# Where GpSimd's three side stores stand: one loop with a comparison, and tiles 16 and 23 in 5, 48 and 75 partitions

## The chip, the cores and the metric

The kernel runs on one core of a Trainium2 chip. The metric is the device time of one execution in microseconds; for the kernel before it is the median of three runs, 207.06 us (207.04 to 207.12). The core has five engines with programs of their own: TensorE (PE in the profile), VectorE (DVE), ScalarE (ACT), GpSimd (POOL) and SyncE (SP). They meet through semaphores. Transfers between the chip's main memory (HBM) and the on-chip memory (SBUF, 128 partitions) are issued by SyncE and by GpSimd and carried out by 16 DMA engines.

## The reference

```python
"x": (16, 512, 1024) float32, "weight": (1024, 768) float32, "add_value": (16, 512, 768) float32, scale = 0.1

return (scale * np.matmul(x, weight) + add_value).astype(np.float32)
```

Read as one matrix, x has 8192 rows. 33.6 MB of x, 25.2 MB of add_value and 3.1 MB of the weight are read, and 25.2 MB are written.

## The kernel before, in words

The 8192 rows are 64 tiles of 128 rows, one row a partition. Sixteen consecutive rows belong to one partition (`R = 16`), so a tile range such as "(8, 8)", tiles 8 to 15, is one contiguous piece of HBM for each partition. A name like x(40,8) below is the entry `("x", 40, 8)` of the list `STREAM` (L22): the load of tiles 40 to 47 of x. a(40,8) loads the same tiles of add_value, and o(40,8) would store them.

SBUF holds x in 16 tile slots (`xs`), and add_value in 32 slots (`ao`), which are also where the results are made and from where they are stored. Tile t uses slot t mod 16 of `xs` and slot t mod 32 of `ao`. The weight comes in through slots 24 to 31 of `ao`.

Five programs run side by side.

- SyncE (`sync_engine`, L97) issues the entries of `STREAM` in the order written there, each after the waits that it needs: a load of x into a used slot waits until ScalarE and GpSimd have cast what was in it (`by_act`, `by_pool`); a load of add_value waits for the load of add_value before it (`a_sem`), for the store that frees its slots (`o_sem`), and, where its slots hold the tile `PAIR.start`, for GpSimd's stores (`aside_sem`, L125); a store waits for the second last store before it (`o_sem`) and until its last tile is finished (`made`). SyncE does one entry after the other, so an entry that waits holds up all entries behind it.
- ScalarE and GpSimd (`mover`, L150) cast x to bf16, each one half of every tile. A turn of their loop is 16 tiles, in four groups of four tiles; each group is eight casts on each of the two engines. The group waits for its load (`x_sem`) and until its buffer `va` has been transposed (`turned`).
- VectorE (`vector_engine`, L166) transposes two tiles at a time (`turn`, `xt` from `va`) and finishes two tiles at a time (`finish`: scale times product plus add_value, in place in `ao`). In its order the transposes of tiles 40 and 41 stand between the finishing of tiles 36, 37 and that of tiles 38, 39.
- TensorE (`tensor_engine`, L218) multiplies tile by tile, four tiles a turn, and has four accumulators.

Around the change: GpSimd's program before is the loop of `mover` for the first two turns (tiles 0 to 31), a wait until tile 15 is finished (`made`, L246), three stores over GpSimd's own DMA queue (`store_pair`, L93), an alignment of the instruction address (`addr_align`, L249), and the loop again for the last two turns. The three stores carry tiles 8 and 15 (`PAIR = slice(8, 16, 7)`) in 6, 98 and 24 partitions (`BY_POOL`: partitions 122 to 127, 0 to 97 and 98 to 121). SyncE stores the tiles between them, 9 to 14, as o(9,6), and tiles 16 to 23 as o(16,8). The load that takes the slot of tile 8 again, and so waits for `aside_sem`, is a(40,8).

`addr_align(HALF_BLOCK, offset=PAST, max_nops=0)` places the instruction that follows it at 4 past a multiple of 64 instructions. ScalarE and VectorE have one ahead of their programs (L235).

Of the kernel before, what the change touches and what calls it, by code (L numbers as in the profile page):

```python
# [10 lines left out]
R = 16  # L11
X_SLOTS = 16
A_SLOTS = 32
# [6 lines left out]
HALF_BLOCK, PAST, SYNC_AT = 64, 4, 4  # L20
# [1 line left out]
STREAM = [  # L22
# [6 lines left out]
]  # L29
FIRST, ENDING = (0, 8), 48  # L30
PAIR, TURN_AT = slice(8, 16, 7), 2
BY_POOL = [(122, 6), (0, 98), (98, 24)]


@with_exitstack
def kernel(
# [8 lines left out]
    nc = tc.nc  # L45
# [8 lines left out]
    T = M // P  # L54
# [5 lines left out]
    out_v = out_f.rearrange("(g p t) n -> p g t n", p=P, t=R)  # L60
    w_v = weight.rearrange("(c p r) n -> p c (r n)", p=P, r=2)

    def rows(view, s, n):
        assert s // R == (s + n - 1) // R
        return view[:, s // R, s % R:s % R + n, :]
# [5 lines left out]
    ao = const.tile([P, A_SLOTS, N], fp32, name="ao")  # L71
# [10 lines left out]
    aside_sem = tc.alloc_semaphore("aside")  # L82
    by_act, by_pool, pool_go, turned, casts, done, made = (
        tc.alloc_semaphore(name)
        for name in ("by_act", "by_pool", "pool_go", "turned", "casts", "done", "made"))
    TURNED = MOVE * VA_BUFS
    MADE = TURNED + 2 + MM_BUFS - 2
# [3 lines left out]
        return t % A_SLOTS  # L91

    def store_pair(eng, p, n):  # L93
        assert PAIR.stop <= R and PAIR.stop <= A_SLOTS
        eng.dma_start(out_v[p:p + n, 0, PAIR, :], ao[p:p + n, PAIR, :]).then_inc(aside_sem, 16)  # L95

    def sync_engine(eng):  # L97
        groups, stores, known = 0, [], {}

        def need(sem, value):  # L100
            if known.get(sem, 0) < value:
                eng.wait_ge(sem, value)  # L102
                known[sem] = value

        for at, (op, s, n) in enumerate(STREAM):
# [14 lines left out]
            elif op == "a":  # L120
# [4 lines left out]
                if s <= PAIR.start + A_SLOTS <= last:  # L125
                    need(aside_sem, 16 * len(BY_POOL))
                if s >= A_SLOTS:
# [19 lines left out]
            if op == "x" and n == 2 * MOVE:  # L147
                eng.sem_inc(x_sem[k // MOVE + 1], 16)

    def mover(eng, copy, parity, count, go=None, first=0, turns=T // X_SLOTS):  # L150
        if go is None:
            eng.preload_act_table(mybir.ActivationFunctionType.Copy)  # L152
        with eng.Fori(16 * (first + 1), 16 * (first + turns) + 1, 16) as i:  # L153
            for q in range(X_SLOTS // MOVE):
                eng.wait_ge(x_sem[q], i)
                eng.wait_ge(turned, i + (4 * q - 12) if q < 3 else i)  # L156
                if go is not None:
                    eng.sem_inc(go, 1)  # L158
                k = MOVE * q
                src = xs[:, k:k + MOVE, :].rearrange("p i (c b k) -> p (i c) b k", b=4, k=64)  # L160
                for a in (parity, parity + 2):
                    for b in range(4):
                        copy(va[q % VA_BUFS][32 * b:32 * b + 32, :, a, :],  # L163
                             src[32 * a:32 * a + 32, :, b, :]).then_inc(count, 1)

    def vector_engine(eng):  # L166
        ao_g = ao.rearrange("p (g t) n -> p g t n", t=G)

        def cast_w(s, n):
            eng.wait_ge(w_sem[s // 4], 16)  # L170
            eng.tensor_copy(w_bf[:, s:s + n, :], ao[:, W_AT + s:W_AT + s + n, :]).then_inc(casts, n)  # L171

        def turn(move, half, moves=None):
            if half == 0:
                eng.wait_ge(by_act, moves)
                eng.wait_ge(by_pool, moves)  # L176
            q = 2 * half * KC
            eng.transpose(  # L178
                xt[:, 2 * half:2 * half + 2, :, :].rearrange("p i c m -> p (i c m)"),
                va[move % VA_BUFS][:, q:q + 2 * KC, :, :].bitcast(fp32).rearrange("p c a k -> p (c a k)"),  # L180
            ).then_inc(turned, 2)

        def finish(pair, at, products):
            eng.wait_ge(done, products)
            a = ao_g[:, at, 2 * pair:2 * pair + 2, :]
            q = 2 * (pair % 2)
            eng.scalar_tensor_tensor(  # L187
                a, mm[:, q:q + 2, 0:N], float(scale), a,
                op0=mybir.AluOpType.mult, op1=mybir.AluOpType.add).then_inc(made, 2)

        def group(i, at, last):
            eng.wait_ge(a_sem, i)
            for p in range(4):
                finish(p, at, i + (4 * p - 12) if p < 3 else i)
                if p < 2 or not last:
                    turn(1 if p < 2 else 0, p % 2, i + 8 if p == 2 else i)

        cast_w(0, 4)
        cast_w(4, 4)
        turn(0, 0, 8)  # L200
        turn(0, 1)
        with eng.Fori(16, 2 * T, 16) as i:
            group(i, bass.ds((i // 16 + A_SLOTS // G - 1) % (A_SLOTS // G), 1), False)
        s = slot(T - G) // G
        group(2 * T, slice(s, s + 1), True)
# [12 lines left out]
    def tensor_engine(eng):  # L218
        eng.sem_inc(x_sem[1], 16)
        eng.sem_inc(turned, TURNED)  # L220
        eng.sem_inc(made, MADE)
        eng.wait_ge(casts, KJ)
        with eng.Fori(TURNED + 2, TURNED + 2 + T, XT_TILES) as i:
            for q in range(XT_TILES):
                if q % 2 == 0:
                    eng.wait_ge(turned, i + q if q else i)
                    eng.wait_ge(made, i + q if q else i)
                for j in range(KJ):
                    x2 = xt[:, q, j // 2, :].bitcast(bf16).rearrange("p (m r) -> p r m", r=2)
                    m = product(eng, mm[:, q, :], x2[:, j % 2, :], w_bf[:, j, :], j)  # L230
                if q % 2:
                    m.then_inc(done, 4)


    for eng in (nc.scalar, nc.vector):  # L235
        eng.addr_align(HALF_BLOCK, offset=PAST, max_nops=0)
    s, n = FIRST
    place = dataclasses.replace(xs[:, s:s + n, :], dep_tracking_offset=P * X_SLOTS * K)
    first = nc.sync.dma_start(place, rows(x_v, s, n))
    first.then_inc(x_sem[0], 16)  # L240
    tc.no_tile_sem_insts.add(first.ins.name)
    with tc.tile_critical(no_gpsimd_drain=True):  # L242
        sync_engine(nc.sync)
        mover(nc.scalar, nc.scalar.copy, 0, by_act)
        mover(nc.gpsimd, nc.gpsimd.tensor_copy, 1, by_pool, pool_go, 0, TURN_AT)
        nc.gpsimd.wait_ge(made, MADE + PAIR.stop)  # L246
        for p, n in BY_POOL:
            store_pair(nc.gpsimd, p, n)
        nc.gpsimd.addr_align(HALF_BLOCK, offset=PAST, max_nops=0)  # L249
        mover(nc.gpsimd, nc.gpsimd.tensor_copy, 1, by_pool, pool_go, TURN_AT, T // X_SLOTS - TURN_AT)  # L250
        vector_engine(nc.vector)
        tensor_engine(nc.tensor)
    ctx.close()
# [39 lines left out]
```

## Time and profile before

| | |
|---|---|
| median of three runs | 207.06 us (207.04 to 207.12) |
| the profiled execution, in all | 206.85 us |
| its span, first to last instruction | 205.5 us |
| TensorE busy | 167.5 us, 82% |
| ScalarE, GpSimd busy | 134.7 us, 137.4 us |
| VectorE busy | 98.0 us |
| moved by DMA | 87.04 MB, 424 GB/s over the span |
| granted TensorE clock, mean | 0.986 |

The profile is of one execution. Times in its views count from the start of the span. "q1" is the queue of SyncE's transfers, "q0" that of GpSimd's, "q14" the queue by which engines fetch instructions. A row of the timeline has its start, its length, the engine ("SPq" is the issuing of SyncE), line, operation, what it writes and reads, how many, and in brackets how long the engine had stood idle and what ended that. A row of the DMA issues ends with the size of one transfer and the time from issue to landing. In the table by stretch each row has the stretch, its length, then busy time and count of instructions of PE, PEld, DVE, ACT and POOL, then clock, the DMA engines' mean busy share and what they moved in GB/s.

### The profile page before, as it was taken

What the parts mean: (1) busy time and instruction counts of PE and PEld (TensorE: products, weight loads), DVE (VectorE), ACT (ScalarE), POOL (GpSimd) and SP (SyncE); (2) the same over time, 40 slices, a digit from 0 to 9 for tenths busy, and PEclk for the clock granted to TensorE, in tenths of its full rate; (3) what the DMA queues carried; (4) which work ended last, traced back from release to release, by engine and by line L of the source; (5) the groups of instructions that cost most, each with busy time, mean ns of one, the idle gap of its engine ahead of it and who ended that gap; (6) DMA issues with size and microseconds to landing.
All of it is one profiled execution on the core that took longest, in us unless ns stands there. A gap on an engine that the chain in (4) does not pass through costs nothing.

```text
span 205.5 us, 2223 instructions
## 1 busy us (share of the span) xinstructions
PE 167.5 (82%) x1008; PEld 50.4 (25%) x512; DVE 98.0 (48%) x66; ACT 134.7 (66%) x129; POOL 137.4 (67%) x135
## 2 busy tenths in 40 slices
PE   0000099999999999999999999999999997999900
PEld 0000022233322333223332233332333322333200
DVE  0004525537555555465555555555552853455330
ACT  2049980699999906999999059999991099920000
POOL 0049994699999916999999549999992099930000
PEclk9999999999999999999999999999999999999995
DMA  8989999999999899999999999999999999998997
GB/s 287 427 372 438 440 485 408 392 437 459 446 459 459 357 459 408 408 426 413 455 404 450 431 416 464 434 411 421 440 431 415 437 448 421 493 459 364 423 440 304
DMA packets 4065, 87.04 MB, mean 424 GB/s; under 512 B 480, under 2 KB 480, under 8 KB 1120
## 3 DMA queue, kind: packets, MB, share of 16 engines
q1 hardware_dynamic: 3856, 86.25, 98.1%
q0 software_dynamic: 208, 0.79, 0.9%
q14 instruction: 1, 0.01, 0.0%
HBM read 61.87 MB, written 25.17 MB: 424 GB/s over the span
## 4 chain that ended last, share of the span: by engine, by line
DMA 38%; PE 36%; POOL 10%; ACT 5%; issue 4%; DVE 3%; SPq 1%; POOLq 0%; DVEq 0%; ACTq 0%
PE mm L210 36%; DMA out_dram<-ao 22%; DMA xs<-in_x_dram 15%; POOL va L163 9%; ACT va L163 5%; DVE xt L178 2%; DVE ao L187 1%; POOL out_dram L95 1%; SPq L130 0%; SPq L118 0%; DVEq L176 0%; SPq L102 0%; POOLq L156 0%; POOLq L158 0%; POOLq L153 0%
## 5 line engine op out<-in xcount | busy, mean ns | idle before, releaser
L210 PE MATMUL mm<-w_bf,xt 128*128 128x256 bf16 (+1 forms) x1008 | 167.5, 327 | 28.0 <-DVE xt L178 27.1
L163 POOL CAST va<-xs 32x1024 bf16<-32x1024 f32 x128 | 135.2, 1056 | 44.2 <-DMA xs<-in_x_dram 36.8
L163 ACT CAST va<-xs 32x1024 bf16<-32x1024 f32 x128 | 133.4, 1042 | 45.2 <-DMA xs<-in_x_dram 42.2
L187 DVE SCALAR_TENSOR_TENSOR ao<-mm,ao 128x1536 f32 (+1 forms) x32 | 56.2, 1756 | 72.9 <-PE mm L210 68.9
L208 PEld LDWEIGHTS <-xt 128*128 128x128 bf16 x512 | 50.4, 98 | 144.6 <-issue 116.6
L178 DVE STREAM_TRANSPOSE xt<-va 128x1024 f32<-128x1024 f32 x32 | 39.4, 1234 | 8.4 <-POOL va L163 6.3
L171 DVE CAST w_bf<-ao 128x3072 bf16<-128x3072 f32 x2 | 4.5, 2240 | 18.1 <-DMA ao<-in_weight_dram 18.1
L152 ACT ACT_TABLE_LOAD x1 | 1.3, 1283 | 1.3 <-SPq L242 1.3
L95 POOL DMA_DIRECT2D out_dram<-ao x3 | 2.0, 672 | 0.0
L274 POOL MEMSET const-float32-0.0<- 128x1 f32 x1 | 0.1, 98 | 0.2 <-issue 0.2
L274 POOL MEMSET const-bfloat16-1.0<- 128x1 bf16 x1 | 0.1, 101 | 0.0
L274 POOL MEMSET const-float32-1.0<- 128x1 f32 x1 | 0.1, 98 | 0.0
L274 POOL MEMSET const-uint8-127<- 128x1 uint8 x1 | 0.1, 98 | 0.0
## 6 DMA issues: line engine op xcount, KB each, us to landing
xs<-in_x_dram SPq DMA_DIRECT2D x7, 4096.0 KB, 20.9
ao<-in_add_value_dram SPq DMA_DIRECT2D x6, 3072.0 KB, 15.7
out_dram<-ao SPq DMA_DIRECT2D x3, 3072.0 KB, 27.4
ao<-in_add_value_dram SPq DMA_DIRECT2D x1, 6144.0 KB, 24.2
out_dram<-ao SPq DMA_DIRECT2D x1, 6144.0 KB, 31.2
out_dram<-ao SPq DMA_DIRECT2D x1, 4608.0 KB, 14.9
xs<-in_x_dram SPq DMA_DIRECT2D x2, 2048.0 KB, 21.0
ao<-in_weight_dram SPq DMA_DIRECT2D x2, 1536.0 KB, 16.8
```

The costliest lines, as they stand in the source:

```text
L95: eng.dma_start(out_v[p:p + n, 0, PAIR, :], ao[p:p + n, PAIR, :]).then_inc(aside_sem, 16)
L152: eng.preload_act_table(mybir.ActivationFunctionType.Copy)
L163: copy(va[q % VA_BUFS][32 * b:32 * b + 32, :, a, :], src[32 * a:32 * a + 32, :, b, :]).then_inc(count, 1)
L171: eng.tensor_copy(w_bf[:, s:s + n, :], ao[:, W_AT + s:W_AT + s + n, :]).then_inc(casts, n)
L178: eng.transpose(xt[:, 2 * half:2 * half + 2, :, :].rearrange("p i c m -> p (i c m)"), va[move % VA_BUFS][:, q:q + 2 * KC, :, :].bitcast(fp ...
L187: eng.scalar_tensor_tensor(a, mm[:, q:q + 2, 0:N], float(scale), a, op0=mybir.AluOpType.mult, op1=mybir.AluOpType.add).then_inc(made, 2)
L208: eng.ldweights(x_j, tile_position=(0, 0))
L210: m = eng.add_instruction(mybir.InstMatmult(start_tensor_calc=(j == 0), stop_tensor_calc=(j == KJ - 1), tile_size=(P, P), tile_position=(0 ...
L274: nc = _bacc.Bacc("TRN2", target_bir_lowering=False, num_devices=1)
```

## The change

GpSimd's program becomes one loop over the four turns. At the end of each turn the counter is compared with 32, the value in the second turn; there, and only there, GpSimd waits and issues its three stores. The wait is now for tile 23, and the stores carry tiles 16 and 23, in partitions 123 to 127, 0 to 47 and 48 to 122. SyncE's list stores tiles 8 to 15 whole and tiles 17 to 22 in place of 16 to 23. The load that waits for `aside_sem` becomes a(48,8). The alignment between the two loops goes, and GpSimd gets one ahead of its program, as ScalarE and VectorE have.

```diff
@@ STREAM
-    ("x", 32, 8), ("a+", 16, 16), ("o", 0, 8), ("o", 9, 6), ("a", 32, 8), ("x", 40, 8),
-    ("a", 40, 8), ("x", 48, 8), ("o", 16, 8), ("o", 24, 8), ("a", 48, 8), ("x", 56, 4),
+    ("x", 32, 8), ("a+", 16, 16), ("o", 0, 8), ("o", 8, 8), ("a", 32, 8), ("x", 40, 8),
+    ("a", 40, 8), ("x", 48, 8), ("o", 17, 6), ("o", 24, 8), ("a", 48, 8), ("x", 56, 4),
...
-PAIR, TURN_AT = slice(8, 16, 7), 2
-BY_POOL = [(122, 6), (0, 98), (98, 24)]
+PAIR, TURN_AT = slice(16, 24, 7), 2
+BY_POOL = [(123, 5), (0, 48), (48, 75)]
@@ store_pair
-        assert PAIR.stop <= R and PAIR.stop <= A_SLOTS
-        eng.dma_start(out_v[p:p + n, 0, PAIR, :], ao[p:p + n, PAIR, :]).then_inc(aside_sem, 16)
+        assert PAIR.start // R == (PAIR.stop - 1) // R and PAIR.stop <= A_SLOTS
+        at = slice(PAIR.start % R, (PAIR.stop - 1) % R + 1, PAIR.step)
+        eng.dma_start(out_v[p:p + n, PAIR.start // R, at, :], ao[p:p + n, PAIR, :]).then_inc(aside_sem, 16)
@@ mover
-    def mover(eng, copy, parity, count, go=None, first=0, turns=T // X_SLOTS):
+    def mover(eng, copy, parity, count, go=None):
...
-        with eng.Fori(16 * (first + 1), 16 * (first + turns) + 1, 16) as i:
+        with eng.Fori(16, 16 * (T // X_SLOTS) + 1, 16) as i:
...
+            if go is not None:
+                with eng.If(i == 16 * TURN_AT):
+                    eng.wait_ge(made, MADE + PAIR.stop)
+                    for p, n in BY_POOL:
+                        store_pair(eng, p, n)
@@ the programs
-    for eng in (nc.scalar, nc.vector):
+    for eng in (nc.scalar, nc.gpsimd, nc.vector):
         eng.addr_align(HALF_BLOCK, offset=PAST, max_nops=0)
...
-        mover(nc.gpsimd, nc.gpsimd.tensor_copy, 1, by_pool, pool_go, 0, TURN_AT)
-        nc.gpsimd.wait_ge(made, MADE + PAIR.stop)
-        for p, n in BY_POOL:
-            store_pair(nc.gpsimd, p, n)
-        nc.gpsimd.addr_align(HALF_BLOCK, offset=PAST, max_nops=0)
-        mover(nc.gpsimd, nc.gpsimd.tensor_copy, 1, by_pool, pool_go, TURN_AT, T // X_SLOTS - TURN_AT)
+        mover(nc.gpsimd, nc.gpsimd.tensor_copy, 1, by_pool, pool_go)
```

## The prediction

> **What bounds the kernel now.** I read the page's head and its queues first, then the busy time by stretch, then SyncE's issues beside the landing of each transfer, then the chain of waits. The queues:
>
> ```profile
> span 205.5 us, 2223 instructions
> ...
> PE 167.5 (82%) x1008; PEld 50.4 (25%) x512; DVE 98.0 (48%) x66; ACT 134.7 (66%) x129; POOL 137.4 (67%) x135
> ...
> q1 hardware_dynamic: 3856, 86.25, 98.1%
> q0 software_dynamic: 208, 0.79, 0.9%
> q14 instruction: 1, 0.01, 0.0%
> ```
>
> The packets of SyncE's queue (q1) fill 98.1% of sixteen engines' time over the whole span; GpSimd's three stores are the 0.9%. No compute engine is near that (TensorE has 82%). By stretch (second column the length, then busy time and count of PE, PEld, DVE, ACT, POOL, then clock, DMA share, GB/s):
>
> ```profile
> 92.00:112.00 20.00, 19.90 (x124) 5.98 (x62) 10.83 (x9) 19.54 (x20) 19.05 (x20) 1.00 1.00 427
> ...
> 172.00:192.00 20.00, 18.82 (x116) 5.63 (x58) 11.57 (x8) 9.07 (x9) 9.31 (x9) 1.00 1.02 442
> ```
>
> The DMA share is about 1 with GpSimd's stores in flight (first row) and without them. TensorE is nearly as full (19.9 of 20 us in the first row), so it has to be asked which of the two sets the end. For that I lay SyncE's issues (start, time until the last of the row is issued) beside the landings (last number of a row: us from issue):
>
> ```profile
> 96.02 0.34 SPq L130 DMA_DIRECT2D ao<-in_add_value_dram  x1
> 96.47 0.84 SPq L118 DMA_DIRECT2D xs<-in_x_dram  x1
> 116.40 0.33 SPq L130 DMA_DIRECT2D ao<-in_add_value_dram  x1
> 116.82 0.39 SPq L118 DMA_DIRECT2D xs<-in_x_dram  x1
> ...
> 144.80 0.34 SPq L130 DMA_DIRECT2D ao<-in_add_value_dram  x1
> ...
> 159.64 38.10 SPq L143 DMA_DIRECT2D out_dram<-ao  x3
> ...
> 186.96 10.78 SPq L143 DMA_DIRECT2D out_dram<-ao  x2
> ...
> 197.41 0.33 SPq L143 DMA_DIRECT2D out_dram<-ao  x1
> ```
>
> ```profile
> ao<-in_add_value_dram SPq DMA_DIRECT2D x1, 3072.0 KB, 14.4
> xs<-in_x_dram SPq DMA_DIRECT2D x1, 4096.0 KB, 24.0
> ao<-in_add_value_dram SPq DMA_DIRECT2D x1, 3072.0 KB, 11.4
> xs<-in_x_dram SPq DMA_DIRECT2D x1, 4096.0 KB, 20.6
> ...
> out_dram<-ao SPq DMA_DIRECT2D x1, 6144.0 KB, 31.2
> out_dram<-ao SPq DMA_DIRECT2D x1, 4608.0 KB, 14.9
> out_dram<-ao SPq DMA_DIRECT2D x1, 1536.0 KB, 8.1
> ```
>
> In this order they are a(32,8) and x(40,8), issued at 96.02 and 96.47; a(40,8) and x(48,8), issued at 116.40 and 116.82; o(32,16), o(48,12) and o(60,4), issued at 159.64, 186.96 and 197.41. Issue plus landing: a(32,8) 110.4, x(40,8) 120.5, a(40,8) 127.8, x(48,8) 137.4, o(32,16) 190.8, o(48,12) 201.9, o(60,4) 205.5. From each landing to the next: 7.3 us for 3072 KB, 9.6 for 4096, 11.0 for 4608, 3.65 for 1536, which is 2.40 to 2.45 us per 1024 KB each time. After a(40,8) the list still holds 32,768 KB, and 205.5 - 127.8 = 77.7 us is 2.43 us per 1024 KB. So the transfers land one behind the other at one rate and the queue never runs dry: a(40,8) is issued 4.1 us before x(40,8) ahead of it lands, o(48,12) 3.9 us before o(32,16) does, o(60,4) 4.5 us before o(48,12). The bytes in the queue set the end, and the time of an issue matters only where it comes later than the landing ahead of it. How long before that a transfer must be issued is bounded by the first one of the program, which met an empty queue, in the chain of waits:
>
> ```profile
> 0.74 12.05 DMA xs<-in_x_dram
> ...
> 97.65 18.69 DMA out_dram<-ao
> ...
> 195.57 1.76 DVE ao L187
> ```
>
> 12.05 us for 4096 KB is 2.3 us over the 9.7 of a full queue. So a lead of 2.3 us is enough, and the smallest here is 3.9. The chain also shows a(40,8) released by the landing of GpSimd's stores (97.65 + 18.69 = 116.34). That is a real wait of SyncE, but with 4.1 us of transfers still queued it delays nothing.
>
> **The change, part by part.**
>
> *The bytes.* 768 KB go over GpSimd's queue in both kernels, and all else over SyncE's. SyncE's store (9,6) grows by 768 KB to (8,8), its store (16,8) shrinks by 768 KB to (17,6). Up to a(40,8) the queues carry 768 KB more, 0.75 x 2.43 = 1.8 us, so a(40,8) lands at 129.6; after it they hold 32,000 KB, 31.25 x 2.43 = 75.9 us. Together 205.5: nothing.
>
> *The wait for GpSimd's stores.* It moves from a(40,8) to a(48,8), which is issued at 144.80, behind o(16,8). What becomes late for a(40,8) now is its predecessor's landing, a(32,8) at 110.4 + 1.8 = 112.2, still 10 us ahead of x(40,8), which lands at 122.3. Queued behind a(48,8) on SyncE are x(56,4), x(60,4), a(56,8) and the last stores; GpSimd's stores, issued at the same place in its program, are down by 116.34 + 1.8 at the latest, about 118, so this wait is over before it is reached. Nothing.
>
> *x(40,8) lands 1.8 us later.* This is the one place where TensorE can feel the change:
>
> ```profile
> 120.68 21.82 POOL L163 CAST va<-xs 32x1024 bf16<-32x1024 f32 x20 [4.95 <-DMA xs<-in_x_dram]
> ...
> 129.51 1.25 DVE L178 STREAM_TRANSPOSE xt<-va 128x1024 f32<-128x1024 f32 x1 [1.05 <-POOL va L163]
> 131.91 1.76 DVE L187 SCALAR_TENSOR_TENSOR ao<-mm,ao 128x1536 f32 x1 [1.15 <-PE mm L210]
> ...
> 174.49 20.97 PE L210 MATMUL mm<-w_bf,xt 128*128 128x512 bf16 x126 [1.13 <-DVE xt L178]
> ```
>
> The casts of tiles 40 to 43 start at 120.68 on that landing, their transpose waits for the casts and ends at 130.76, 1.15 us before TensorE is through with tile 39 (131.91). Shifted by 1.8 it ends at 132.6: TensorE stalls 0.65 us. Cover: at 174.49 TensorE waits 1.13 us for tiles 56 to 59, whose load x(56,4) is behind as many bytes as before and lands at the same time. The 0.65 goes into that wait (1.13 becomes about 0.5), and the last product, DVE's last step at 195.57 and the store at 197.41 stay. Without that cover o(48,12) would have 3.9 - 0.65 = 3.2 us of lead, still over 2.3. Nothing.
>
> *GpSimd's program.* The wait for tile 23 and the three stores:
>
> ```profile
> 90.31 1.76 DVE L187 SCALAR_TENSOR_TENSOR ao<-mm,ao 128x1536 f32 x1 [1.40 <-PE mm L210]
> ...
> 96.23 2.01 POOL L95 DMA_DIRECT2D out_dram<-ao  x3
> 98.29 1.03 POOL L163 CAST va<-xs 32x1024 bf16<-32x1024 f32 x1
> ```
>
> Tiles 22 and 23 are finished at 92.07, the stores start at 96.23, so the stricter wait holds nothing. Behind it stand the casts of tiles 32 to 47, as before. Three stores stay, 2.01 us together, and the next cast follows 0.05 us later. The comparison runs four times; no row shows one. Bounds: nothing (the sequencer runs ahead of the casts) and the 2.01 us of the three stores. I take nothing, since the loop's own branch into the third turn fits into those 0.05 us. Cover: GpSimd waits 4.95 us for x(40,8) (above). The one instruction fetch inside the span (q14) may fall away:
>
> ```profile
> q14 instruction: 1, 0.01, 6.4%
> ```
>
> In the queues from 98.4 to 98.7 it is 6.4% of sixteen engines over 0.3 us: 0.31 us on one engine. Gain between 0 and 0.31, 0.02 on the mean of sixteen. I take 0.02.
>
> *The split 6, 98, 24 against 5, 48, 75.* It decides which engine gets which of the 768 KB, and the last engine sets the end. The fall of the DMA share at the end:
>
> ```profile
> 204.00:204.25 0.25, 0.00 (x0) 0.00 (x0) 0.00 (x0) 0.00 (x0) 0.00 (x0) 0.50 0.58 246
> 204.25:204.50 0.25, 0.00 (x0) 0.00 (x0) 0.00 (x0) 0.00 (x0) 0.00 (x0) 0.50 0.70 295
> 204.50:204.75 0.25, 0.00 (x0) 0.00 (x0) 0.00 (x0) 0.00 (x0) 0.00 (x0) 0.50 0.12 49
> ```
>
> Full engines to the end would have done the 0.25 x (0.58 + 0.70 + 0.12) = 0.35 us after 204.00 by 204.35, not 204.75. So evenness is worth 0 to 0.4 us, and a worse split could cost about as much again. I take -0.1: 48 is a multiple of 16 and can be shared evenly, of the old three counts none is.
>
> The Trainium skill ("DMA: Bandwidth & Descriptors", on why a DMA increments its semaphore by 16) has a rule for it: a transfer uses the largest number of engines up to 16 that divides its partitions, from GpSimd with a cursor that goes round. By it the old split puts 9 partitions on ten engines and 3 on two, the new one 9 on four, 8 on eleven and 4 on one; at 6 KB a partition (36 KB for 6), 0.23 us on one engine at the rate above, this would take up to 0.2 us from the end instead of my 0.1. The fall above agrees that the engines end unevenly; no view here shows them singly.
>
> *Sum.* 205.5 - 0.02 - 0.1 = 205.4 us of span. The profiled execution took 206.85 in all, 1.35 over its span, and the median of the runs is 207.06, 0.21 above it. So 207.06 - 0.12 = **206.95**.
>
> **The rivals.**
>
> *The removed wait was worth its time (faster).* For it: the chain runs through it, and a(40,8) could go 116.4 - 112.2 = 4.2 us earlier: 202.9. Against it: the even landings. A gain needs an idle queue, and there is none.
>
> *The split evens the end altogether (faster).* The whole 0.4 us, 206.6.
>
> *The loop fetches its own code again (slower).* If the loop lies across the edge of what GpSimd keeps, each taken branch waits for instructions, and a fetch queues behind data. Price per turn: from 0.31 us to the landing of the smallest transfer in the full queues:
>
> ```profile
> out_dram<-ao POOLq DMA_DIRECT2D x1, 36.0 KB, 7.4
> ...
> 37.58 34.95 POOL L163 CAST va<-xs 32x1024 bf16<-32x1024 f32 x32 [4.26 <-DMA xs<-in_x_dram]
> ...
> 65.98 1.23 DVE L178 STREAM_TRANSPOSE xt<-va 128x1024 f32<-128x1024 f32 x1
> ```
>
> The row at 37.58 holds the casts of tiles 8 to 23, 34.95 / 32 = 1.09 us each. Those of tiles 16 to 19, the first of the second turn, end with its 24th at 63.8, 2.2 us before their transpose at 65.98: a stall under 2.2 us is hidden, and from there on it decides. At 7.4 us TensorE stops for 5.2, of which the wait before tile 56 takes back 1.1; the other 4.1 bring o(48,12) to 191.1, and with the 2.3 us until its data flow, to 193.4, which is 2.5 after the queue ran out at 190.8: 207.06 + 2.5 = 209.6. Against it: the fetch at 98.4 to 98.7 held nothing, the cast at 98.29 having started.
>
> The Trainium skill ("Runtime: NRT & Kernel Launch", instruction fetch mechanics) says that a taken branch whose target is outside the resident window forces a fetch before execution goes on. By it this rival's time would come about if the one loop lies across that window; no row shows such a stall in the kernel before.
>
> *TensorE's stall is not absorbed and the queue is touched (slower).* The full 1.8 us at o(48,12) leaves 2.1 us of lead, 0.2 under 2.3; with a split as much worse as it could be better, 207.06 + 0.2 + 0.4 = 207.7.
>
> **How the numbers follow.** Forecast 0.76 (206.95, own range 206.65 to 207.4); removed wait 0.03; full evening 0.10; code fetch 0.05; late TensorE with a worse split 0.06. A difference under 0.2% (0.4 us) counts as no change, what a measurement here can tell. Faster: 0.03 + 0.10 = 0.13, and 0.01 of the forecast's edge, 0.14. Slower: 0.11. Same: 0.75. The range, 206.5 to 207.5, takes in the full evening and most of a worse split; the two large cases stay outside.
>
> **What would show it.** Right: landings still 2.43 us per 1024 KB from 96 on; a(40,8) issued near 112; x(40,8) down near 122; a TensorE wait of about 0.6 us near tile 40 and about 0.5 before tile 56; no q14 packet; the last store issued near 197.4. Wrong: a gap of over 0.2 us between GpSimd's last cast of one turn and its first of the next where the load has landed (the comparison or a fetch costs), a transfer issued after the one ahead has landed, or a DMA share well under 1 between 96 and 200.

## The result, and the profile after

The changed kernel takes **208.41 us** (median of six runs, 207.71 to 209.02); the kernel before took 207.05 beside it (207.01 to 207.12). The ratio is 1.0068, with a 95% interval of 1.0056 to 1.0081: slower by 1.4 us, where 206.95 was forecast. The profiled execution took 208.26 us, of which 206.6 are its span; before it was 206.85 and 205.5. So 1.1 us were added inside the span and 0.3 outside it, before the first instruction or after the last (1.66 us in place of 1.35).

The head of the page and its queues:

```profile
span 206.6 us, 2225 instructions
...
q1 hardware_dynamic: 3856, 86.25, 97.7%
q0 software_dynamic: 192, 0.79, 0.9%
```

SyncE's queue moves the same 86.25 MB in as many packets, and the queue is still nearly full over the whole span, 97.7% where it was 98.1%. The instruction fetch (q14) is gone, as forecast. SyncE's issues in the timeline, and for the same transfers the time from issue to landing:

```profile
96.22 0.34 SPq L131 DMA_DIRECT2D ao<-in_add_value_dram  x1
96.67 0.76 SPq L119 DMA_DIRECT2D xs<-in_x_dram  x1
113.28 0.33 SPq L131 DMA_DIRECT2D ao<-in_add_value_dram  x1
115.83 0.33 SPq L119 DMA_DIRECT2D xs<-in_x_dram  x1
...
160.22 38.13 SPq L144 DMA_DIRECT2D out_dram<-ao  x3
187.57 0.34 SPq L144 DMA_DIRECT2D out_dram<-ao  x1
198.02 0.33 SPq L144 DMA_DIRECT2D out_dram<-ao  x1
```

```profile
ao<-in_add_value_dram SPq DMA_DIRECT2D x1, 3072.0 KB, 17.0
xs<-in_x_dram SPq DMA_DIRECT2D x1, 4096.0 KB, 26.1
ao<-in_add_value_dram SPq DMA_DIRECT2D x1, 3072.0 KB, 16.8
xs<-in_x_dram SPq DMA_DIRECT2D x1, 4096.0 KB, 23.9
...
out_dram<-ao SPq DMA_DIRECT2D x1, 6144.0 KB, 31.8
out_dram<-ao SPq DMA_DIRECT2D x1, 4608.0 KB, 15.3
out_dram<-ao SPq DMA_DIRECT2D x1, 1536.0 KB, 8.5
```

Issue plus landing, beside the landing before and the shift that the prediction gave it:

| transfer | before | after | shift | forecast shift |
|---|---|---|---|---|
| a(32,8) | 110.4 | 113.2 | 2.8 | 1.8 |
| x(40,8) | 120.5 | 122.8 | 2.3 | 1.8 |
| a(40,8) | 127.8 | 130.1 | 2.3 | 1.8 |
| o(32,16) | 190.8 | 192.0 | 1.2 | 0 |
| o(48,12) | 201.9 | 202.9 | 1.0 | 0 |
| o(60,4) | 205.5 | 206.5 | 1.0 | 0 |

The lateness that 768 KB do not explain is there at the landing of a(32,8), 1.0 us; it is 0.5 at x(40,8) and a(40,8), and 1.0 to 1.2 at the last stores. So the first place to look is between 96 and 113 us. There the profile by stretch shows a dent in one microsecond. First row the kernel before, second the changed one (columns as in the prediction: DMA share and GB/s at the end):

```profile
102.00:103.00 1.00, 1.00 (x9) 0.31 (x4) 1.00 (x2) 0.97 (x2) 0.94 (x2) 1.00 0.96 406
```

```profile
102.00:103.00 1.00, 1.00 (x8) 0.32 (x4) 1.00 (x2) 0.97 (x2) 0.94 (x2) 1.00 0.62 240
```

A slice this short counts a packet where it starts, so it wobbles; over the six microseconds around it the two read

```profile
100.00:106.00 6.00, 6.00 (x39) 1.82 (x19) 3.00 (x3) 5.85 (x7) 5.64 (x7) 1.00 1.03 438
```

```profile
100.00:106.00 6.00, 6.00 (x39) 1.86 (x19) 3.30 (x3) 5.85 (x7) 5.64 (x7) 1.00 0.98 415
```

438 GB/s before, 415 after. These rows wobble too: six microseconds later the kernel before reads

```profile
106.00:112.00 6.00, 5.95 (x38) 1.77 (x19) 3.71 (x3) 5.85 (x7) 5.70 (x6) 1.00 0.98 419
```

so the rate only says where to look. What is special about this place is that two stores run at once. GpSimd's stores are issued at 96.28 and their packets begin near 101; before, SyncE's store o(9,6) was down at 101.74, so they met it for some 0.7 us. Now SyncE has the larger o(8,8) there, which is down at 104.0, and they run beside it for about 3 us.

The packets of the trace are surer than the rate. Call a packet late by the time that it takes over the median of the packets of its queue and size. In 100 to 106 us one packet of GpSimd's was late by 0.70 us, and two of SyncE's on another engine by 0.15 and 0.39; the sum over all packets is 1.40 us, and 0.35 in the kernel before. Shared by sixteen engines the difference is only 0.07 us. Of the 1.0 us at a(32,8) some 0.3 is a matter of order: before, 20 of GpSimd's packets, 0.12 MB, ran after that landing, and now none do. The rest is unevenness. A transfer has landed when the last of the sixteen engines is through: of o(60,4) fifteen engines were down by 205.8 us and the last at 206.5. Nearly every packet starts 3 or 4 ns before the end of the one ahead of it on its engine, so the packets can be strung together into sixteen engines by their starts and ends. The engine of those two SyncE packets is the one that ends last: its packets are 0.54 us too long between 100 and 125 us, and 0.76 between 150 and 175, of which 0.70 is one packet at 174.6, where the queue goes over from a(56,8) to o(32,16). So only 0.54 of its 1.3 us lie in the overlap of the two stores or just behind it. Why it was hit a second time was not shown; in one of the kernels below (f3) too an engine that fell behind near 103 us was hit again, by 0.76 us at 138. At the end of the changed kernel the DMA share falls like this:

```profile
204.25:204.50 0.25, 0.00 (x0) 0.00 (x0) 0.00 (x0) 0.00 (x0) 0.00 (x0) 0.50 1.15 492
204.50:204.75 0.25, 0.00 (x0) 0.00 (x0) 0.00 (x0) 0.00 (x0) 0.00 (x0) 0.50 0.13 49
204.75:205.00 0.25, 0.00 (x0) 0.00 (x0) 0.00 (x0) 0.00 (x0) 0.00 (x0) 0.50 0.35 148
205.00:205.25 0.25, 0.00 (x0) 0.00 (x0) 0.00 (x0) 0.00 (x0) 0.00 (x0) 0.50 0.00 0
205.25:205.50 0.25, 0.00 (x0) 0.00 (x0) 0.00 (x0) 0.00 (x0) 0.00 (x0) 0.50 0.12 49
205.50:205.75 0.25, 0.00 (x0) 0.00 (x0) 0.00 (x0) 0.00 (x0) 0.00 (x0) 0.50 0.12 49
```

49 GB/s in a slice of 0.25 us is 12 KB, one packet of o(60,4): from 205.00 on it is the last packets of single engines that are waited for. Before, the last such packet was in the slice at 204.50.

### The profile page after: what moved, and what is told of

The parts are those of the page before. It is cut to its first block, busy times and chain, and to the rows that moved or that the text cites. A ratio compares the mean times of both kernels' runs of the same rounds, so it can differ in the third digit from the quotient of the medians.

```text
span 206.6 us, 2225 instructions
## 1 busy us (share of the span) xinstructions
PE 167.4 (81%) x1008; PEld 50.3 (24%) x512; DVE 98.1 (47%) x66; ACT 134.7 (65%) x129; POOL 137.6 (67%) x135
## 3 DMA queue, kind: packets, MB, share of 16 engines
q1 hardware_dynamic: 3856, 86.25, 97.7%
## 4 chain that ended last, share of the span: by engine, by line
DMA 39%; ACT 22%; PE 16%; POOL 10%; issue 6%; DVE 3%; ACTq 0%; POOLq 0%; DVEq 0%; SPq 0%
DMA xs<-in_x_dram 39%; ACT va L164 22%; PE mm L216 16%; POOL va L164 10%; DVE xt L184 2%; DVE ao L193 1%; ACTq L154 0%; ACTq L157 0%; DVEq L182 0%; POOLq L154 0%; DVEq L193 0%; POOLq L159 0%; POOLq L167 0%; POOLq L157 0%; DVEq L190 0%
```

## The experiments

The change has three parts: the loop form of GpSimd's program, the other tiles with SyncE's shifted queue, and the split. Each group below says what its kernels change against which of the two kernels. GB/s is that of the stretch 100 to 106 us in each kernel's own profile, and "late" the lateness of the packets that start in that stretch, in sum, which tells the kernels apart better than the rate does.

### The split

The changed kernel with the old split, and the kernel before with the new one:

```diff
-BY_POOL = [(123, 5), (0, 48), (48, 75)]
+BY_POOL = [(122, 6), (0, 98), (98, 24)]
```

```diff
-BY_POOL = [(122, 6), (0, 98), (98, 24)]
+BY_POOL = [(123, 5), (0, 48), (48, 75)]
```

> The changed kernel (one loop, tiles 16 and 23) with the three pieces of before, 6, 98 and 24 partitions. If the split is the cause: 207.0 to 207.3 us, and the runs within 0.2 us of each other. If the loop, its alignment or the choice of tiles is the cause: 208.2 to 208.6 with about 1 us between the runs, as the changed kernel.

> The kernel before with the pieces 5, 48 and 75 and nothing else changed. If the split is the cause: 207.7 to 209.0 us, about 1 us between the runs. If the program or the tiles are: 207.0 to 207.2.

Two further ones: a single store of 128 partitions (`BY_POOL = [(0, 128)]`) in the changed kernel, and the old split in another order, `[(0, 98), (98, 24), (122, 6)]`, in the kernel before, which gives the same shares to other DMA engines.

> The changed kernel with one store of all 128 partitions in place of three: 8 partitions for each of the 16 engines in every run. If what matters is that one engine is behind and needs the light share (3 partitions of 8 before, 5 x 0.23 us less work): 207.7 to 208.3, the runs within 0.2 of each other, since nothing moves from run to run. If what matters is only that the shares of the changed kernel are uneven: 206.8 to 207.1. If the program is the cause: 208.2 to 208.6, about 1 us between the runs.

> The kernel before with its own three pieces issued in another order, 98, 24, 6. By the rule of the going round cursor the two engines with 3 partitions become the 15th and 16th from the cursor, where before they are the 5th and 6th; ten engines have 9 as before. If it matters which engine is light: 207.6 to 208.4, the runs within 0.2 of each other. If only the sizes of the pieces or their unevenness matter: 207.0 to 207.2.

Later the single store was put into the kernel before as well:

> The kernel before with one store of 128 partitions, 8 on every engine, in place of 6, 98, 24. If one engine is behind by itself in every kernel and the light share hides it: 208.0 to 208.4, as the changed kernel with one store (208.19), the last engine over 1 us behind the rest at the end, and the rest together. If the choice of tiles made that engine late: 206.8 to 207.1.

| kernel | median | ratio to before | GB/s | late, us |
|---|---|---|---|---|
| new, old split (e1) | 208.77 | 1.0091 (1.0074 to 1.0108) | 389 | 4.68 |
| old, new split (e2) | 207.03 | 1.0007 (0.9998 to 1.0017) | 428 | 0.06 |
| new, one store (e3) | 208.19 | 1.0059 (1.0042 to 1.0076) | 413 | 0.25 |
| old, other order (e4) | 208.40 | 1.0074 (1.0057 to 1.0091) | 427 | 0.10 |
| old, one store (g4) | 208.11 | 1.0058 (1.0041 to 1.0076) | 431 | 0.05 |

In the old kernel the new split costs little (0.2 us by the medians, and the interval takes in no change), so it isn't what made the change 1.4 us slower; in the new kernel it is even the better of the two. But e4 and g4 are 1.6 and 1.0 us slower than the kernel before beside them (206.81 and 207.07), with hardly a late packet between 100 and 106 us: this loss is of another kind. In e3 too the packets of that stretch are not late, although its one store runs beside o(8,8) for some 2.5 us; why it was spared was not shown. The end of e3 shows the other kind:

```profile
204.25:204.50 0.25, 0.00 (x0) 0.00 (x0) 0.00 (x0) 0.00 (x0) 0.00 (x0) 0.50 0.14 49
204.50:204.75 0.25, 0.00 (x0) 0.00 (x0) 0.00 (x0) 0.00 (x0) 0.00 (x0) 0.50 0.01 0
204.75:205.00 0.25, 0.00 (x0) 0.00 (x0) 0.00 (x0) 0.00 (x0) 0.00 (x0) 0.50 0.12 49
205.00:205.25 0.25, 0.00 (x0) 0.00 (x0) 0.00 (x0) 0.00 (x0) 0.00 (x0) 0.50 0.12 49
205.25:205.50 0.25, 0.00 (x0) 0.00 (x0) 0.00 (x0) 0.00 (x0) 0.00 (x0) 0.50 0.00 0
205.50:205.75 0.25, 0.00 (x0) 0.00 (x0) 0.00 (x0) 0.00 (x0) 0.00 (x0) 0.50 0.12 49
205.75:206.00 0.25, 0.00 (x0) 0.00 (x0) 0.00 (x0) 0.00 (x0) 0.00 (x0) 0.50 0.00 0
206.00:206.25 0.25, 0.00 (x0) 0.00 (x0) 0.00 (x0) 0.00 (x0) 0.00 (x0) 0.50 0.12 49
```

With one store of 128 every DMA engine gets eight of GpSimd's partitions, as the Trainium skill has it ("DMA: Bandwidth & Descriptors", on why a DMA increments its semaphore by 16: the largest number of engines up to 16 that divides the partitions); the packets agree. All engines have the same bytes then, yet fifteen of them are down by 205.2 in both e3 and g4, and one at 207.1 and 206.6. That engine's packets in e3 are 0.63 us too long in sum between 150 and 175 us and 0.53 between 175 and 200, those of the others by at most 0.07. By the packets the old split leaves two engines with three of GpSimd's partitions and the new one leaves one engine with four, where the others have eight or nine. The strings show where the light share falls. One engine is slow in each of these kernels: from 90 us to the end its packets are late by 1.8 to 2.1 us in sum (the changed kernel, e2, e3, e4, f4, h1). It has three of GpSimd's partitions with the old split (f1 and h2 below), four with the new one, eight in e3 and nine in e4, and in e3 and e4 it is the one that ends last. So the light share hides its lateness, and the time rises when that share is gone (e3, g4) or goes to other engines (e4). It also tells the two splits apart: a packet of one partition takes 0.23 us, and with four of them the slow engine is the last by a little in e2, f4 and h1 as well. No trace gives the engine's number.

### The loop and the tiles, one at a time

The loop alone (one loop with its comparison and its alignment, as in the diff of the change, with tiles 8 and 15 and SyncE's old queue), and the tiles alone (two loops as before, `PAIR = slice(16, 24, 7)` and the new `STREAM`), each with both splits:

> The one loop with its comparison and the alignment ahead of it; tiles 8 and 15 and the pieces 6, 98, 24 stay as before. If the program is what makes the changed kernel slow: 208.2 to 208.8 us. If the choice of tiles is (SyncE's store of 8 whole tiles stands in the queue where GpSimd's stores come in): 206.8 to 207.2, as the kernel before.

> The two loops of before with tiles 16 and 23 and SyncE's list of the changed kernel; pieces 6, 98, 24. If the choice of tiles is the cause: 208.2 to 208.9, as the changed kernel with these pieces (208.77). If the program is: 206.8 to 207.2.

> As the run before, with the pieces 5, 48, 75. If the choice of tiles is the cause: 207.7 to 209.0 with about 1 us between the runs, as the changed kernel, from which it then differs in the program alone. If the program is: 206.9 to 207.2, as the kernel before with these pieces (207.03).

> The one loop with tiles 8 and 15 and the pieces 5, 48, 75. If the program is the cause: 207.7 to 209.0. If the choice of tiles is: 206.9 to 207.2. If neither is alone (each of this run and the run before near 207.0): the loop and the tiles act together.

| kernel | median | ratio to before | GB/s | late, us |
|---|---|---|---|---|
| loop, old split (f1) | 207.22 | 1.0015 (1.0005 to 1.0024) | 438 | 0.06 |
| loop, new split (f4) | 207.49 | 1.0028 (1.0018 to 1.0038) | 433 | 0.28 |
| tiles, old split (f2) | 208.80 | 1.0095 (1.0078 to 1.0112) | 392 | 3.75 |
| tiles, new split (f3) | 208.09 | 1.0057 (1.0040 to 1.0073) | 415 | 1.95 |

The tiles with their shifted queue make most of the loss, in a kernel that still has its two loops, and with them packets are late between 100 and 106 us (of the kernels with these tiles and GpSimd's stores at this place, only e3 has hardly any). The loop adds 0.3 us without late packets, and the new split another 0.3 (f4 against f1).

### The queue or the place in HBM

The tiles change two things: where GpSimd's stores write, and what SyncE's queue carries ahead of a(32,8). First the queue alone. GpSimd keeps tiles 8 and 15; SyncE stores two tiles more ahead of a(32,8):

```diff
-    ("x", 32, 8), ("a+", 16, 16), ("o", 0, 8), ("o", 9, 6), ("a", 32, 8), ("x", 40, 8),
-    ("a", 40, 8), ("x", 48, 8), ("o", 16, 8), ("o", 24, 8), ("a", 48, 8), ("x", 56, 4),
+    ("x", 32, 8), ("a+", 16, 16), ("o", 0, 8), ("o", 9, 6), ("o", 16, 2), ("a", 32, 8), ("x", 40, 8),
+    ("a", 40, 8), ("x", 48, 8), ("o", 18, 6), ("o", 24, 8), ("a", 48, 8), ("x", 56, 4),
```

> The kernel before, with GpSimd storing tiles 8 and 15 in 6, 98, 24 as it did; only SyncE's queue carries 768 KB more ahead of a(32,8), as in the changed kernel: o(16,2) is issued right ahead of a(32,8), and o(18,6) takes the place of o(16,8). If the shift of the queue by 1.8 us is what costs: 208.2 to 208.9 us, as with tiles 16 and 23 and these pieces (208.8). If it is where GpSimd's stores go: 206.8 to 207.3.

Then the place alone: in the kernel before, GpSimd's stores write where tiles 16 and 23 go (`out_v[p:p + n, 1, 0:8:7, :]`), and in the changed one where tiles 48 and 55 go (`out_v[p:p + n, 3, at, :]`).

> The kernel before with one thing changed: GpSimd's three stores write the data of tiles 8 and 15 to the place of tiles 16 and 23 in the output, 6 MiB further on, where SyncE's o(16,8) later writes too; the places of tiles 8 and 15 are left unwritten. Issue order, sizes and waits are as before. If the place in HBM is what costs, with SyncE's store (9,6) in flight at the old place: 208.2 to 208.9 and packets stretched near 101 to 104 us. If the shift of the queue or the place in SBUF costs: 206.8 to 207.2.

> The changed kernel with GpSimd's stores going to the place of tiles 48 and 55, 18 MiB behind SyncE's o(8,8), instead of 6 MiB; SyncE's o(48,12) writes there later, and the places of tiles 16 and 23 are left unwritten. If only the distance of 6 MiB is bad: 207.0 to 207.6. If any place away from SyncE's store in flight is bad, or the shift of the queue is: 207.7 to 208.9 as the changed kernel.

The queue alone gave 208.93 us, ratio 1.0088 (1.0067 to 1.0109), with 373 GB/s and 12.39 us late. The place alone left the old kernel at 207.13, 1.0017 (0.9994 to 1.0040), with 431 GB/s and 0.08 us late, though two of its ten runs took 208.34 and 208.81, more than any of the kernel before beside it (206.80 to 207.94); and the new one at 208.48, 1.0073 (1.0044 to 1.0102), with 408 and 2.20. It is the queue. The queue alone differs from the changed kernel in one more thing: its additional store o(16,2) moves in packets of 6 KB where o(8,8) has 24 KB, which may be why its packets are so much later than those of f2 (3.75 us) for the same time.

```profile
100.00:106.00 6.00, 6.00 (x38) 1.85 (x19) 2.91 (x2) 5.53 (x7) 5.68 (x6) 1.00 1.02 373
```

This row of the queue alone shows how such a loss hides: the DMA share is 1.02, every engine is busy, and 373 GB/s pass where 438 did. A packet that is held up counts as busy.

### Store beside store, or a later queue

The queue shifts, so SyncE's store runs longer beside GpSimd's, but also every load comes later. To tell these apart, GpSimd's stores are moved in time. In the changed kernel they go one group of tiles later, behind the first group of the third turn, with both splits:

```diff
-            if go is not None:
-                with eng.If(i == 16 * TURN_AT):
+                if go is not None and q == 0:
+                    with eng.If(i == 16 * (TURN_AT + 1)):
```

> The changed kernel with GpSimd's three stores issued one group of tiles later, after its casts of tiles 32 to 35 (near 107 us, not 96.28): SyncE's store o(8,8) has then landed (104.0) and its queue holds only the loads a(32,8) and x(40,8). Theory A (what costs is the data of GpSimd's stores beside the data of a store of SyncE's): the stretched packets between 100 and 106 us go, no engine falls behind there, and the time comes back to 207.0 to 207.6. Theory B (what costs is that 768 KB more of SyncE's stores lie ahead of a(32,8), so every load from there on is later): 208.2 to 208.6, as the changed kernel. Theory C (the stores of GpSimd cost the same wherever they run): 208.2 to 208.6 too, with the stretch moved to 110 to 118 us.

> The same later stores with the old split 6, 98, 24. With the new tiles and stores at the old place this split gave 208.8, 0.4 to 0.6 over the new split. Theory A: 207.0 to 207.6, and the two splits within 0.3 us of each other, as they are with the old tiles. Theory B or C: 208.6 to 209.0.

In the loop with the old tiles and the old queue (the 207.22 of f1) they go one group earlier, `if go is not None and q == 2:` in the second turn:

> GpSimd's one loop, but with the old tiles 8 and 15, the old queue of SyncE and the old split 6, 98, 24, and the stores issued one group of tiles earlier, after the casts of tiles 24 to 27 (near 88 us): their data now run beside SyncE's o(0,8) and o(9,6), which end at 95.4 and 101.7. With the stores at the old place this kernel had 207.22. Theory A: the overlap of stores is then longer than in the changed kernel, the packets are stretched between 90 and 100 us, 208.2 to 209.2. Theory B: the queue of SyncE is the old one, 207.0 to 207.5. Theory C: 207.0 to 207.5.

| kernel | median | ratio to before | GB/s | late, us |
|---|---|---|---|---|
| new, stores later (h1) | 207.50 | 1.0021 (1.0011 to 1.0031) | 426 | 0.13 |
| new, stores later, old split (h2) | 207.20 | 1.0011 (1.0000 to 1.0021) | 438 | 0.12 |
| old tiles in a loop, stores earlier (h4) | 210.03 | 1.0135 (1.0112 to 1.0159) | 384 | 12.02 |

h1's GpSimd and h4's stretch:

```profile
99.72 5.43 POOL L164 CAST va<-xs 32x1024 bf16<-32x1024 f32 x5
105.10 1.95 POOL L96 DMA_DIRECT2D out_dram<-ao  x3
107.10 5.41 POOL L164 CAST va<-xs 32x1024 bf16<-32x1024 f32 x5
```

```profile
100.00:106.00 6.00, 6.00 (x39) 1.77 (x19) 2.91 (x2) 5.88 (x6) 5.64 (x7) 1.00 1.02 384
```

With the new queue and its later loads the time comes back once the stores are issued at 105.10, when SyncE's o(8,8) is down (103.5 in h1) and its queue holds loads only. GpSimd's packets then run from 109 to 122 us in h1 and to 123 in h2, and those of 106 to 125 us are not late in either (-0.08 and -0.05 us in sum). The two splits are 0.3 us apart, about the one partition more on the slow engine. With the old queue the time goes up by 2.8 us once the stores run beside o(0,8) and o(9,6). So it is the store of GpSimd's queue beside a store of SyncE's that costs, and not the later queue. h4 lost more than was expected of it: its packets are late by 16.4 us in sum between 92 and 106 us, and by 13.4 a second time near 135 us, long after GpSimd's last packet (103.4) and after its engines had ended a(32,8) up to 2.4 us apart. That was not followed, so how much of the 2.8 us is the overlap itself stays open.

### The time outside the span

Over all runs the time less the span falls into two heaps without overlap: 1.29 to 1.41 us for each kernel with two loops, 1.47 to 1.75 for each with one loop. Three runs look for what makes it: the alignment alone in the kernel before, the changed kernel without it, and the kernel before with its two loops but the stores behind the comparison at the end of the first loop's turns.

```diff
-    for eng in (nc.scalar, nc.vector):
+    for eng in (nc.scalar, nc.gpsimd, nc.vector):
```

> The kernel before with one line of the change alone: GpSimd too gets the alignment of the instruction address ahead of its program. In every run so far the time outside the span (the run's time less its span) is 1.29 to 1.41 us for kernels with GpSimd's two loops and 1.47 to 1.75 for those with one loop. First theory (the alignment ahead of the program is what lengthens the part outside the span): 1.5 to 1.65 us outside, 207.2 to 207.4 in all. Second theory (the one loop with its comparison does): 1.3 to 1.4 us outside, 207.0 in all.

```diff
-    for eng in (nc.scalar, nc.gpsimd, nc.vector):
+    for eng in (nc.scalar, nc.vector):
```

> The changed kernel without the alignment ahead of GpSimd's program; loop, comparison, tiles and split stay. First theory (the alignment): 1.3 to 1.4 us outside the span, 208.0 to 208.3 in all. Second theory (the loop with its comparison): 1.5 to 1.7 us outside, 208.2 to 208.6 in all. In both the span stays at 206.2 to 207.4 us, because nothing in SyncE's queue changes.

```diff
+            if go is not None and first == 0:
+                with eng.If(i == 16 * TURN_AT):
...
-        nc.gpsimd.wait_ge(made, MADE + PAIR.stop)
-        for p, n in BY_POOL:
-            store_pair(nc.gpsimd, p, n)
```

> The kernel before, its two loops kept, but with the three stores behind a comparison of the counter at the end of each turn of the first loop, as the changed kernel has them behind one in its single loop. First theory (the comparison, or the stores behind it, makes the 0.26 us outside the span): 1.5 to 1.7 us outside, 207.1 to 207.4 in all. Second theory (the single loop does, wherever the stores are): 1.3 to 1.4 us outside, 206.9 to 207.1 in all. In both the span is 205.4 to 205.9 us.

Outside the span the three have 1.33, 1.60 and 1.32 us (medians). In all they take 206.90, 208.88 and 206.94 us, ratios 0.9998 (0.9988 to 1.0007), 1.0087 (1.0059 to 1.0115) and 1.0004 (0.9994 to 1.0013). So neither the alignment nor the comparison costs anything that can be measured; the 0.26 us go with the single loop. What the chip does in them lies where no profile of these runs looks, and stays open. No kernel tried here is faster than the one before, clear of the noise.

## Why the prediction was wrong, step by step

*The bytes: the step that failed.* "Together 205.5: nothing" took one rate, 2.43 us per 1024 KB, for all that goes through the sixteen engines, whichever queue it comes from and whatever runs beside it. The prediction's own row of 92 to 112 us, with GpSimd's stores in flight at a DMA share of 1, seemed to say so, but in that row the two stores met for only 0.7 us. The term should have been: 768 KB more of a SyncE store reach some 2 us further into GpSimd's, and store beside store costs. Measured, the tiles alone cost 1.1 us (f3, new split) and 1.9 us (f2, old split) in all against the kernel before beside them, 206.95. By the ratios, the loop (f1), then the new split (f4), then the tiles (the changed kernel) bring 0.3, 0.3 and 0.8 us. No rival had this term, and so the range ended 0.9 us short. The rate did not even have to fall: the mean lost under 0.1 us between 100 and 106, and the rest is one late engine. That the overlap in time is what matters is shown by moving the stores (h1, h2); why a late engine is hit again after the overlap (0.76 us in the changed kernel's profile) stays open.

*GpSimd's program: nothing forecast, 0.3 us measured, and not where it was looked for.* Inside the span the step was right: the stores start at 96.28 and the next cast follows 0.05 us behind them,

```profile
96.28 1.95 POOL L96 DMA_DIRECT2D out_dram<-ao  x3
98.28 2.12 POOL L164 CAST va<-xs 32x1024 bf16<-32x1024 f32 x2
```

and m1 shows the comparison to be free. But the prediction carried the 1.35 us around the span over unchanged, and the single loop makes them 1.6. With the 1.1 us of span, which hold the tiles and the split, this is the whole difference of 1.4.

*The split: wrong in sign, and too small in kind.* It was priced at 0 to 0.4 us either way from the evenness of the end, and taken as a gain of 0.1. As a choice between these two splits the size holds and the sign does not: the new one is 0.2 to 0.3 us slower where the stores do not overlap (e2, f4 against f1, h1 against h2), one partition more on the slow engine. By the Trainium skill's rule that the prediction cites it would have taken up to 0.2 us from the end; none of these runs shows such a gain, since the sixteen engines are not equally fast. But what a split can do is larger: 1.0 to 1.6 us when the light share is gone or elsewhere (g4, e4), and 0.4 to 0.7 us when two stores overlap (e1 against the changed kernel, f2 against f3).

*The wait for GpSimd's stores: right.* It left a(40,8), which now goes at 113.28 in place of 116.40, on the landing of a(32,8); the prediction had 112.2. a(48,8) was issued at 145.35, with GpSimd's stores long down (the last at 113.1). The 3.1 us that a(40,8) gained bought nothing, and the rival that the removed wait is worth 4.2 us is out.

*x(40,8) and TensorE: right in kind, short in size.* The rows of TensorE:

```profile
124.80 6.66 PE L216 MATMUL mm<-w_bf,xt 128*128 128x512 bf16 x39
133.15 41.78 PE L216 MATMUL mm<-w_bf,xt 128*128 128x512 bf16 x252 [1.69 <-DVE xt L184]
175.10 20.97 PE L216 MATMUL mm<-w_bf,xt 128*128 128x512 bf16 x126 [0.17 <-DVE xt L184]
```

It waits 1.69 us for tile 40, not 0.65: x(40,8) came 2.3 us later and not 1.8, and TensorE was through with tile 39 at 131.46 and not at 131.91. And the wait before tile 56 took in what it had, from 1.13 to 0.17. The last store goes 0.6 us later than before, at 198.02, but 4.9 us ahead of the landing of o(48,12), so TensorE delays nothing. This and the missing fetch (no q14, no gap behind GpSimd's turns) put the rivals of the late TensorE and of the code fetch out, although 207.7 came nearest.

*What would have shown it in time.* The list of signs named a DMA share well under 1. In the clearest case, the queue alone, the share was 1.02; the sign is in the GB/s beside it.

## What to carry to other kernels

When transfers bound a kernel, don't take it that bytes can be moved along a queue at no cost: check what will then run beside what. Here the side queue's stores were free beside the main queue's loads and not beside its stores. Read GB/s next to the DMA share, because a held-up packet counts as busy, compare packets with their like rather than rates of a few microseconds, and look for the last of the sixteen engines, because the transfer lands with it. And compare the time outside the span as well as the span: a program's form can change it.

## What the runs showed of the hardware

- Stores of GpSimd's queue beside a store of SyncE's stretch single packets, by up to 0.7 us in the changed kernel and 1.5 in e1. In sum the packets of 100 to 106 us are late by 1.4 to 12.4 us in eight of the nine kernels where the two run side by side for some 2 us or more (0.25 in e3, the ninth), and by at most 0.35 in the other eleven. Beside SyncE's loads there was no stretch (h1, h2: -0.08 and -0.05 us in 106 to 125). The Trainium skill ("DMA: Bandwidth & Descriptors", rules for kernel authors) says that spreading transfers over issuing engines brings no bandwidth, since all share the same 16 engines and interleave; the runs agree (the DMA share is about 1 with GpSimd's stores and without), and show that with two stores it takes some away. Which part of the chip is contended was not shown.
- With equal bytes on all sixteen DMA engines one of them ends 1.4 to 1.9 us after the rest (g4, e3); in e3 its packets are late by 1.2 us in SyncE's transfers of 150 to 200 us, long after GpSimd's last packet has ended (109.7 us). With three or four of GpSimd's partitions on it in place of eight or nine, at 0.23 us each, most of this is hidden.
- The form of GpSimd's program, one loop or two, moves the time outside the span by 0.26 us; an alignment and a comparison do not.
